# Second layer: the next heads' keys and values prepared in the middle of a unit instead of at its end, and half of the key copies moved to GpSimd

## The chip, the cores and the metric

The kernel runs on one core of one Trainium2 chip. The metric is the device time of one execution in microseconds, taken as the median of several runs. Beside these runs one execution was profiled; all rows below come from it.

## The reference

Two layers work on 1024 latent tokens and 256 context tokens of width 1024. The first (windowed attention and a gated MLP) is not touched here. The second is multi-head latent attention with 16 heads, and only the latent tokens go on from it:

```python
def mla_keys_values(kv_a, k_pe, kv_norm, w_kvb, row, col):
    kv = (rms_norm(kv_a, kv_norm) @ w_kvb).reshape(B_, L, C_HEADS, C_NOPE + C_V)
    k_nope, v = kv[..., :C_NOPE], kv[..., C_NOPE:]
    ...
    k = jnp.concatenate([k_nope, jnp.broadcast_to(k_pe, ...)], axis=-1)

def block_attention(q, k, v):          # 1024 queries, 1280 keys, 16 heads
    s = jnp.einsum('bqhd,bkhd->bhqk', qblk, k).astype(jnp.float32) * scale
    p = jax.nn.softmax(s, axis=-1)
    return jnp.einsum('bhqk,bkhd->bqhd', p, v)
```

Each head has 64 key columns of its own and 32 rotary ones that all heads share, and 64 value columns. All numbers are float32; a product is made of a high part and a rest (hi and lo) of each factor.

## The kernel before

The attention of the second layer is a loop over 64 **units** (plus three turns that finish late parts). A unit is one head and 256 queries: 8 head pairs, 4 query groups, 2 heads, so units 2m and 2m+1 share the queries of a group. Each turn of the loop walks through `ORDER1`, a list of short names, and each name puts its instructions at the end of each engine's queue. The order within TensorE, VectorE, ScalarE and GpSimd is this written order; the DMA queue of SyncE is ordered by the scheduler. The names, for unit n:

- S0 to S3: scores against the 1024 latent keys, into two PSUM tiles `s0` and `s1` of 1024 columns (one for each 128 queries, one buffer each). S4: scores against the context keys, into `sx`. K: the rotary part, added to `s0` and `s1`; it ends them.
- X0, X1, X2, P0, P1: VectorE takes the maxima of `s0`, `s1` and `sx` and makes the exponent's bias.
- E0 to E3: ScalarE's exponentials, from PSUM to `prob`. E0 reads `s0` and E1 reads `s1`, which frees them for the next unit.
- T0 to T4: TensorE transposes `prob` of the unit before, 512 columns at a time, into a PSUM bank called `tm`; a copy takes each to SBUF (`pt`). By `TURNS` T0 and T4 are copied by VectorE, the rest by ScalarE.
- A0, I, U, C: the products with the values and the normalisation, for earlier units.
- B and R (even units): queries of the next group, projected into a `tm` bank (B), then ScalarE makes `qa` from it and VectorE its rest (R).
- **D and L**: the preparation of later heads. `prep_pair` prepares the keys of the next head pair in four turns out of eight: the first splits the weights, the next three project 512, 512 and 256 columns (D) and evacuate them (L). `prep_v` prepares values for four heads in six turns out of sixteen: one splits weights, five project into a bank (D) and copy it out (L).

The tag `tm` has two banks. Transposes, B and D take them in turn, and whoever takes one waits for the readers of what lay there two allocations ago.

The keys of a head lie twice in `kh` (in partitions 0 to 63 and 64 to 127), and their rest once in `kl`, in a ring of two head pairs. In the evacuation of a key projection ScalarE copies the bank to both halves of `kh` for both heads, four copies, and VectorE subtracts `kh` from the bank to give `kl`, two operations.

Of the kernel before, what the change touches and what calls it, by code (L numbers as in the profile page):

```python
# [7 lines left out]
F32 = mybir.dt.float32  # L8
# [9 lines left out]
D = 1024  # L18
# [21 lines left out]

PAIR, VALUES = (2, 3, 4, 5, 8, 9, 11, 13), (1, 6, 7, 10, 12, 14)
WQ = 'VGG'
ORDER1 = 'S0 S1 T0 T1 I C S2 S3 K X0 T2 S4 T3 X2 P0 E0 B X1 P1 E2 R A0 E1 T4 D E3 U L'.split()
AVS = ((0, 5),), ((5, 10),)
TURNS = 'VAAAV'
KPE = {3: [0], 5: [1]}
# [6 lines left out]
class Kernel:  # L53
# [1083 lines left out]
    def prep_pair(self, hp):  # L1137

        nc, i, c1 = self.nc, self.i, self.c1
        raws = (self.raw(i["wkv_k"][:, hp * P:(hp + 1) * P].unsqueeze(1), [P, 1, P]), self.raw(i["wq_n"][hp], [P, 2, P]))  # L1140
        yield
        w = self.wsplit(c1, raws[0], 1, ("V", WQ[0]))
        self.wq[hp] = self.wsplit(c1, raws[1], 2, ("V", WQ[1]))
        yield
        ring = self.kring[hp % 2]
        kvh, kvl = self.kvh.unsqueeze(1), self.kvl.unsqueeze(1)
        for g0, gn in GROUPS:
            ps = self.project(w, self.split(kvh, kvl), g0, gn)
            yield
            c = slice(g0, g0 + gn)  # L1150
            src = [ps[64 * e:64 * e + 64] for e in range(2)]
            for e in range(2):
                for r in (0, 64):
                    nc.scalar.copy(ring[e][0][r:r + 64, c], src[e])  # L1154
            for e in range(2):
                nc.vector.tensor_tensor(ring[e][1][0:64, c], src[e], ring[e][0][0:64, c].bitcast(F32), op=ALU.subtract)  # L1156
            yield

    def prep_q(self, hp, qg):
# [25 lines left out]
    def layer1_attention(self):  # L1185
# [159 lines left out]
        with self.tc.manual_schedule(engines={E.PE, E.Activation, E.DVE, E.Pool}):  # L1345
            for n in range(N + 3):
                odd = n % 2
                for op in ORDER1:
                    o, a = op[0], int(op[1:] or 0)
# [255 lines left out]
```

## Time and profile before

| what | value |
|---|---|
| runs | 1546.64 to 1549.77 us, median of three 1547.48 us |
| the profiled execution | 1542.2 us, of which the span of the profile is 1540.3 us |
| TensorE matmul, busy share of the span | 1428.8 us, 93% |
| VectorE, ScalarE, GpSimd | 890.1 us (58%), 748.5 us (49%), 454.2 us (29%) |
| the 64 units of the second layer | K of the first at 810.8 us, K of the last at 1428.4 us |

The profile lists busy time for each engine, and for each group of instructions the idle time of its engine just before it with the instruction whose end released it. TensorE is the busiest by far, so its idle times in the loop, and the times at which its granted clock is below full speed, are what to look at first.

### The profile page before, as it was taken

To read this page: it belongs to the slowest core of one execution; us is meant where nothing else is said; L and a number is where in the kernel's file an instruction comes from. 1 tells how busy PE (TensorE), PEld (TensorE's weight loads), DVE (VectorE), ACT (ScalarE), POOL (GpSimd) and SP (SyncE) were. 2 spreads that over 40 slices of the span, in tenths; PEclk is the share of its full clock that TensorE was granted. 3 is DMA by queue.
4 is the path that set the end of the run, shared out by engine and by line. 5 is a ranking of instruction groups with operands and counts; after the bars stand their busy time and mean duration, and the time that the engine had idled before them with its cause. 6 is when DMAs were issued, how large, how long until landed. Compare 5 with 4: busy or idle time off the path is not lost.

```text
span 1540.3 us, 23388 instructions
## 1 busy us (share of the span) xinstructions
PE 1428.8 (93%) x8849; PEld 1103.3 (72%) x8849; DVE 890.1 (58%) x1692; ACT 748.5 (49%) x1580; POOL 454.2 (29%) x447
## 2 busy tenths in 40 slices
PE   6999999999998899999988898989898989899997
PEld 3767899777665577889866666766676667676776
DVE  5581134366667876534736665656666656577354
ACT  4422310256567544443336665756666666667321
POOL 4343133215557432331642121212121211224100
PEclk9999999999999999999999999999999999999999
DMA  8566311221214656140221010101011101212151
GB/s 338 228 229 255 106 34 30 89 96 57 79 56 151 185 148 197 55 128 30 94 93 47 25 34 24 44 21 33 29 33 32 34 22 35 70 41 91 59 186 69
DMA packets 91466, 138.96 MB, mean 90 GB/s; under 512 B 9089, under 2 KB 67657, under 8 KB 88281
## 3 DMA queue, kind: packets, MB, share of 16 engines
q1 hardware_dynamic: 91208, 137.21, 26.7%
q8 instruction: 69, 1.13, 0.3%
q14 instruction: 45, 0.36, 0.1%
q10 hardware_dynamic: 144, 0.26, 0.0%
HBM read 105.88 MB, written 31.56 MB: 89 GB/s over the span
## 4 chain that ended last, share of the span: by engine, by line
PE 41%; ACT 11%; DVE 4%; issue 4%; DMA 2%; POOL 1%; SPq 0%; DVEq 0%; POOLq 0%; ACTq 0%
PE tm L1275 9%; ACT prob L1265 5%; PE acc L1293 4%; PE s L99 3%; PE s L100 3%; PE s L101 3%; PE s L1227 3%; PE s L1228 3%; ACT kh L1154 3%; PE s L1239 2%; ACT pt L1282 1%; PE b L99 1%; PE b L101 1%; PE b L100 1%; DVE kl L1156 1%
## 5 line engine op out<-in xcount | busy, mean ns | idle before, releaser
L1275 PE MATMUL tm<-ident,prob 128*128 128x128 f32 x1280 | 197.2, 283 | 46.6 <-DVE kl L1156 44.9
L1275 PEld LDWEIGHTS tm<-ident,prob 128*128 128x128 f32 x1280 | 145.6, 142 | 102.0 <-issue 75.0
L1282 ACT COPY pt<-tm 128x512 f32<-128x512 f32 x192 | 112.9, 588 | 213.4 <-PE tm L1275 213.2
L1250 DVE TENSOR_REDUCE peak<-s 128x1 f32<-128x1024 f32 x128 | 156.1, 1219 | 50.3 <-PE s L1239 50.3
L1293 PE MATMUL acc<-pt,v 128*64 128x256 f32 x1280 | 152.9, 384 | 0.1
L1265 ACT ACTIVATE prob<-s,peak 128x1024 f32<-128x1024 f32 x128 | 142.7, 1114 | 12.6 <-DVE peak L1254 10.4
L1284 DVE COPY pt<-tm 128x512 f32<-128x512 f32 x128 | 88.4, 691 | 78.9 <-PE tm L1275 77.2
L1293 PEld LDWEIGHTS acc<-pt,v 128*64 128x64 f32 x1280 | 86.3, 136 | 47.3 <-issue 6.1
L1227 PE MATMUL s<-kh,qa 128*128 128x512 f32 x256 | 114.3, 447 | 5.9 <-ACT prob L1265 4.5
L91 POOL CAST qb<-qa 64x512 fp32r<-64x512 f32 x32 | 19.5, 608 | 319.7 <-ACT qa L1175 319.7
L95 POOL TENSOR_TENSOR w_lo<-raw,w_hi 128x512 fp32r<-128x512 f32 (+1 forms) x60 | 74.2, 1249 | 120.4 <-ACT w_hi L87 85.1
L1228 PE MATMUL s<-kl,qb 128*128 128x512 f32 x256 | 104.4, 408 | 0.0
L99 PE MATMUL b<-h,yh 128*128 128x512 f32 x160 | 64.0, 400 | 3.5 <-ACT yh L87 2.9
L99 PE MATMUL s<-h,w_hi 128*128 128x512 f32 x160 | 63.8, 412 | 2.2 <-ACT qk L379 2.2
L100 PE MATMUL s<-h,w_hi 128*128 128x512 f32 x160 | 63.7, 398 | 0.3 <-DVE h L95 0.3
L100 PE MATMUL b<-h,yh 128*128 128x512 f32 x160 | 63.3, 396 | 0.0
L101 PE MATMUL s<-h,w_lo 128*128 128x512 f32 x160 | 63.0, 395 | 0.0
L101 PE MATMUL b<-h,yl 128*128 128x512 f32 x160 | 62.4, 391 | 0.0
L1265 ACT ACTIVATE prob<-sx,peak 128x256 f32<-128x256 f32 x128 | 60.0, 469 | 0.0
L1227 PEld LDWEIGHTS s<-kh,qa 128*128 128x128 f32 x256 | 50.0, 195 | 13.6 <-ACT prob L1265 5.4
L1228 PEld LDWEIGHTS s<-kl,qb 128*128 128x128 f32 x256 | 50.4, 197 | 6.4
L745 DVE TENSOR_TENSOR pt<-pt,tm 128x512 f32<-128x512 f32 x68 | 42.4, 682 | 21.8 <-ACT mb L736 18.9
(473 smaller groups left out, 3750.4 us busy)
## 6 DMA issues: line engine op xcount, KB each, us to landing
wa<-in_w_ada_dram SPq DMA_DIRECT2D x16, 1024.0 KB, 8.1
x<-in_xs_dram SPq DMA_DIRECT2D x20, 512.0 KB, 6.1
raw<-in_w_dram SPq DMA_DIRECT2D x17, 512.0 KB, 4.0
wa<-in_w_adag_dram SPq DMA_DIRECT2D x8, 1024.0 KB, 6.5
pe<-pe_d SPq DMA_DIRECT2D x128, 64.0 KB, 2.0
raw<-in_w_out_dram SPq DMA_DIRECT2D x10, 512.0 KB, 3.8
yf<-y_d SPq DMA_DIRECT2D x10, 512.0 KB, 6.1
x_d<-x SPq DMA_DIRECT2D x8, 512.0 KB, 4.5
```

The lines of the kernel that those rows point to most:

```text
L95: e.tensor_tensor(lo, src, hi.bitcast(F32), op=ALU.subtract)
L99: mm(out, lhsT=ah, rhs=bh, start=start, stop=False)
L100: mm(out, lhsT=ah, rhs=bl, start=False, stop=False)
L101: mm(out, lhsT=al, rhs=bh, start=False, stop=stop)
L1227: mm(o, lhsT=qa[:, q], rhs=ka[:, k0:k1], start=True, stop=False)
L1228: mm(o, lhsT=qb[:, q], rhs=kb[:, k0:k1], start=False, stop=False)
L1250: nc.vector.reduce_max(m[:, 0, a:a + 1], banks[n, a], axis=AX.X)
L1265: nc.scalar.activation(probs[n][j][:, TL:T] if c else probs[n][j][:, 0:TL], src, AF.Exp, bias=peaks[n][:, 2, j:j + 1], scale=scale, accum_ ...
L1275: nc.tensor.transpose(tp[:, o * P:(o + 1) * P], probs[n][j][:, k * P:(k + 1) * P], self.ident)
L1282: nc.scalar.copy(dst, src)
L1284: nc.vector.tensor_copy(dst, src)
L1293: mm(accs[m][64 * e:64 * e + 64, 0:QG], lhsT=self.v4[hp // 2][:, kt, vc:vc + 64], rhs=pts[2 * m + e][:, kt], start=kt == 0, stop=kt == NT - 1)
```

## The change

In `ORDER1` D moves from behind T4 to between S2 and S3, and L moves from the end of the turn to behind K, ahead of the maxima. In the evacuation of a key projection ScalarE keeps the copies to the lower half of `kh`, one for each head; GpSimd copies the lower half to the upper half, from SBUF to SBUF, behind VectorE's two subtractions in the written order.

```diff
-ORDER1 = 'S0 S1 T0 T1 I C S2 S3 K X0 T2 S4 T3 X2 P0 E0 B X1 P1 E2 R A0 E1 T4 D E3 U L'.split()
+ORDER1 = 'S0 S1 T0 T1 I C S2 D S3 K L X0 T2 S4 T3 X2 P0 E0 B X1 P1 E2 R A0 E1 T4 E3 U'.split()
...
             for e in range(2):
-                for r in (0, 64):
-                    nc.scalar.copy(ring[e][0][r:r + 64, c], src[e])
+                nc.scalar.copy(ring[e][0][0:64, c], src[e])
             for e in range(2):
                 nc.vector.tensor_tensor(ring[e][1][0:64, c], src[e], ring[e][0][0:64, c].bitcast(F32), op=ALU.subtract)
+            for e in range(2):
+                self.hi("G", ring[e][0][64:128, c], ring[e][0][0:64, c].bitcast(F32))
             yield
```

TensorE's queue before, at the end of unit 3 (a unit with a key projection) and the start of unit 4: the last two of T4's four transposes, D into bank `tm_7698`, U, S0, and the transposes T0 and T1.

```order
L1275 MATMUL tm_7692<-ident,prob_7560 128x128
L1275 MATMUL tm_7692<-ident,prob_7561 128x128
L99 MATMUL tm_7698<-kvh,w_hi_7613 128x512
L100 MATMUL tm_7698<-kvl,w_hi_7613 128x512
L101 MATMUL tm_7698<-kvh,w_lo_7614 128x512
L1308 MATMUL acc_7590<-ident,spread_7640 128x128 x2
L1227 MATMUL s_1256_7712<-kh_7091,qa_7579 128x512
L1228 MATMUL s_1256_7712<-kl_7092,qb_7580 128x512
...
L1275 MATMUL tm_7718<-ident,prob_7675 128x128 x4
L1275 MATMUL tm_7724<-ident,prob_7675 128x128 x4
```

T1 of unit 4 (`tm_7724`) takes the bank that D (`tm_7698`) filled. The same projection in the changed kernel stands in the middle of unit 3, behind its T0, T1 and the first half of the scores for `s1`:

```order
L1276 MATMUL tm_7627<-ident,prob_7572 128x128 x4
L1276 MATMUL tm_7633<-ident,prob_7572 128x128 x4
L1228 MATMUL s_1247_7643<-kh_7093,qa_7427 128x512
L1229 MATMUL s_1247_7643<-kl_7094,qb_7428 128x512
L99 MATMUL tm_7646<-kvh,w_hi_7541 128x512
L100 MATMUL tm_7646<-kvl,w_hi_7541 128x512
L101 MATMUL tm_7646<-kvh,w_lo_7542 128x512
...
L1240 MATMUL s_1242_7621<-kc,qc_7429 128x512 x2
L1240 MATMUL s_1247_7643<-kc,qc_7429 128x512 x2
L1276 MATMUL tm_7664<-ident,prob_7573 128x128 x4
L1276 MATMUL tm_7677<-ident,prob_7573 128x128 x4
```

D (`tm_7646`) now takes the bank of T0 (`tm_7627`), T2 (`tm_7664`) that of T1, and T3 (`tm_7677`) takes the one that D filled.

VectorE's queue before, from the second projection of the same pair (unit 4): R's two operations, T4's copy, the two subtractions, T0's copy and the inverses of unit 5, then its maxima.

```order
L1177 TENSOR_TENSOR qa_7786<-tm_7776,qa_7786 64x256 x2
L1284 COPY pt_7717<-tm_7809 128x512
L1156 TENSOR_TENSOR kl_7365<-tm_7815,kh_7364 64x512
L1156 TENSOR_TENSOR kl_7367<-tm_7815,kh_7366 64x512
L1284 COPY pt_7831<-tm_7832 128x4x128
L1299 TENSOR_TENSOR total_7562<-total_7562 128x4
L1301 RECIPROCAL total_7562<-total_7562 128x4
L1250 TENSOR_REDUCE peak_7857<-s_1277_7826 128x1
```

And in the changed kernel, for the third projection (256 columns, unit 5): T0's copy, the inverses, the two subtractions, and the maxima behind them.

```order
L1285 COPY pt_7831<-tm_7832 128x4x128
L1300 TENSOR_TENSOR total_7574<-total_7574 128x4
L1302 RECIPROCAL total_7574<-total_7574 128x4
L1155 TENSOR_TENSOR kl_7365<-tm_7851,kh_7364 64x256
L1155 TENSOR_TENSOR kl_7367<-tm_7851,kh_7366 64x256
L1251 TENSOR_REDUCE peak_7867<-s_1277_7826 128x1
L1249 TENSOR_REDUCE peak_7867<-sx_7875 128x2
```

The subtractions stood behind the last copy of a unit; they now stand between its first copy and its first maximum.

## Rows read from the trace of the kernel before

**Rows 1.** Waits in 800 to 1430 us: engine line, releaser; us total, times, longest.

```profile
PE tm L1275 <- DVE kl L1156: 44.9, 21, 2.6
...
PE tm L99 <- DVE qa L1177: 7.1, 16, 0.5
```

**Rows 2.** Timeline of TensorE around one such wait: start us, us, instruction, [idle, releaser].

```profile
998.17 0.48 PE L99 MATMUL tm<-kvh,w_hi 128*128 128x512 f32 x1
...
1000.10 0.60 PE L1275 MATMUL tm<-ident,prob 128*128 128x128 f32 x4
1003.17 0.83 PE L1275 MATMUL tm<-ident,prob 128*128 128x128 f32 x4 [2.47 <-DVE kl L1156]
...
1004.22 0.63 PE L1228 MATMUL s<-kl,qb 128*128 128x512 f32 x1
```

**Rows 3.** Timeline of ScalarE there.

```profile
999.25 2.35 ACT L1154 CAST kh<-tm 64x512 fp32r<-64x512 f32 x4
```

**Rows 4.** Timeline of VectorE there.

```profile
1001.63 1.39 DVE L1156 TENSOR_TENSOR kl<-tm,kh 64x512 fp32r<-64x512 f32 x2 [2.49 <-ACT kh L1154]
```

**Rows 5.** K by its line: count, duration in ns (least/median/most), first and last start.

```profile
L1239 PE MATMUL s<-kc,qc x256: 489/497/792, 810.8 to 1428.4; 32*128 32x512 f32 x128
```

**Rows 6.** TensorE in units 15 to 17, which prepare no keys or values.

```profile
960.13 0.51 PE L1239 MATMUL s<-kc,qc 32*128 32x512 f32 x4
...
965.25 0.48 PE L1227 MATMUL s<-kh,qa 128*128 128x512 f32 x1
...
966.26 1.03 PE L1275 MATMUL tm<-ident,prob 128*128 128x128 f32 x8
...
967.60 0.39 PE L1227 MATMUL s<-kh,qa 128*128 128x512 f32 x1
...
968.15 0.51 PE L1239 MATMUL s<-kc,qc 32*128 32x512 f32 x4
...
969.80 0.60 PE L1275 MATMUL tm<-ident,prob 128*128 128x128 f32 x4
...
973.75 0.49 PE L1227 MATMUL s<-kh,qa 128*128 128x512 f32 x1
...
976.68 0.50 PE L1239 MATMUL s<-kc,qc 32*128 32x512 f32 x4
```

**Rows 7.** VectorE in unit 16.

```profile
966.90 0.69 DVE L1284 COPY pt<-tm 128x512 f32<-128x512 f32 x1 [0.89 <-PE tm L1275]
...
968.76 1.23 DVE L1250 TENSOR_REDUCE peak<-s 128x1 f32<-128x1024 f32 x1 [0.38 <-PE s L1239]
...
970.73 0.21 DVE L1254 TENSOR_SCALAR peak<-peak 128x1 f32<-128x1 f32 x1
...
973.44 0.86 DVE L1177 TENSOR_TENSOR qa<-tm,qa 64x256 fp32r<-64x256 f32 x2 [1.12 <-ACT qa L1175]
974.33 0.69 DVE L1284 COPY pt<-tm 128x512 f32<-128x512 f32 x1
```

**Rows 8.** ScalarE in unit 16.

```profile
971.06 1.12 ACT L1265 ACTIVATE prob<-s,peak 128x1024 f32<-128x1024 f32 x1
```

**Rows 9.** GpSimd in unit 16.

```profile
973.41 0.61 POOL L91 CAST qb<-qa 64x512 fp32r<-64x512 f32 x1 [8.78 <-ACT qa L1175]
```

**Rows 10.** VectorE and ScalarE around a 256-wide key slot (unit 21) and a value slot (22).

```profile
1027.77 0.86 DVE L1156 TENSOR_TENSOR kl<-tm,kh 64x256 fp32r<-64x256 f32 x2 [1.64 <-ACT kh L1154]
...
1026.23 1.50 ACT L1154 CAST kh<-tm 64x256 fp32r<-64x256 f32 x4
...
1037.54 0.59 ACT L1134 COPY v<-tm 128x512 f32<-128x512 f32 x1 [0.38 <-PE tm L101]
```

**Rows 11.** TensorE's projection of values in unit 22.

```profile
1036.56 0.35 PE L99 MATMUL tm<-wvh,kvh 128*128 128x256 f32 x1 [0.44 <-DVE qa L1177]
```

**Rows 12.** Stretches: length, busy us and count by engine, granted clock, DMA.

```profile
950.00:1050.00 100.00, 92.19 (x659) 68.66 (x658) 63.19 (x112) 61.23 (x137) 18.17 (x26) 0.97 0.10 31
...
1350.00:1400.00 50.00, 50.00 (x377) 37.73 (x375) 36.36 (x61) 36.05 (x81) 16.02 (x19) 1.00 0.20 59
```

## The prediction

> **What bounds the kernel now.** I read the page's shares first: TensorE is busy for nine tenths of the span, so the question is what it waits for in the second layer's loop. The list of waits for that stretch names two things that belong to the preparation of later heads [rows 1]: T1 waits for the subtractions `kl`, 44.9 us in 21 waits, and D itself waits for R's `qa`, 7.1 us in 16. The 21 are the key projections (7 head pairs, three each). The timeline of one of them shows why: TensorE has done T0 and stands 2.47 us before T1 [rows 2], because T1's bank is the one that D filled, and that bank is read last by `kl`, which starts only behind all four `kh` copies [rows 3, 4], which stand behind the four exponentials. The reader should see that `kl` starts 0.03 us after the last copy, not after the first one that it needs.
>
> How much the preparation costs in all comes from the starts of K. The first lies at 810.8 us, the last at 1428.4 [rows 5]: 617.6 us for 63 intervals. A unit that prepares nothing takes 8.02 us when odd and 8.53 when even [rows 6], together 32 x 8.53 + 31 x 8.02 = 521.6. A 512-wide key projection is three matmuls of 512 columns; four scores of that size take 1.01 us from S0 to T0 [rows 6], so three take 0.70 to 0.75, and I take 0.70. A value step streams as many columns; a 256-wide key projection half of them, 0.36: 14 x 0.70 + 15 x 0.70 + 7 x 0.36 = 22.8. That leaves 73 us; about 2 of it I put down to the loop's first and last units, which differ. So **71 us are lost around the preparation**: 52.0 listed waits; 37 x 0.2 = 7.4, since a wait costs more than is listed (T0 to T1 took 3.07 us [rows 2]; eight transposes and two scores take 1.34 and two scores 0.55 [rows 6], so four transposes need 0.40, and 2.67 was lost where 2.47 is listed); and 11.6 that remain. The remainder is TensorE's clock: behind the wait a score matmul takes 0.63 us where it takes 0.39 elsewhere [rows 2, 6], and the mean granted clock over 100 us of such units is 0.97, so between its two levels (1.2 and 2.4 GHz), against 1.00, the upper level throughout, where no keys are prepared [rows 12].
>
> **The change, part by part.** I replay a unit with times from S0's start, from unit 16 (S0 at 965.25): T0's copy ends at 2.34, the second half of the scores for `s1` starts at 2.35, K at 2.90, the first maximum 0.61 behind K, T3 at 4.55, the next S0 at 8.50 [rows 6, 7] (8.02 for an odd unit).
>
> *D between S2 and S3.* It takes T0's bank, so it waits for T0's copy. From the end of the last `kl` to T1 the trace has 0.15 us [rows 2, 4]; so D starts at 2.49, not 2.35: 0.14 lost in each of 36 slots with a projection. This is the least certain small term; from zero to 0.3.
>
> *512-wide keys (14 slots).* D takes 0.70, so K, T2, S4 and T3 come 0.84 later, T3 at 5.39. T3 now takes D's bank. From D's start to a reader on ScalarE is 0.98 us (1036.56 to 1037.54, same columns [rows 10, 11]): `kh` starts at 3.47, two copies at 0.59 end at 4.65 [rows 3], `kl` runs from 4.68 to 6.07 [rows 4], T3 starts at 6.22: **a wait of 0.83** in place of the old 2.5 to 2.6. The maxima are queued behind `kl`: X0 starts at 6.10, where 4.35 was possible. Its bias is ready 2.18 later (8.28) and E0, which in the trace starts about 0.1 behind the bias [rows 7, 8], has read `s0` at 8.38 + 1.12 = 9.5. The next S0 comes at 8.02 + 0.84 + 0.83 = 9.69 in an odd unit: the later maxima just fit. This is the cover, and it has under 0.1 us to spare when 0.15 is needed for the signal; each 0.1 more on the chain costs 1 us over ten odd units.
>
> *Four of the 14 are even*, with R. Its subtraction starts 2.38 behind E0 [rows 7, 8], at 10.76, ends at 11.62 and frees B's bank for the next T0 at 11.77; that T0 is due at 8.50 + 1.67 + 1.01 = 11.18, so 0.59 late, and T1 waits for T4's copy, which stands behind R's subtraction (0.69 and the signal: 12.49 against 12.17), 0.32 more. Such a unit loses 0.97 + 0.9.
>
> *256-wide keys (7 slots, all odd).* Two copies of 0.375 and two subtractions of 0.43 [rows 10]: T3's bank is free at 4.92, T3 is due at 5.05. Only D's 0.14 is lost. *Values (15 steps):* one copy, long before T3; 0.14 each. In even units the wait for `qa` goes, since D no longer takes B's bank.
>
> *GpSimd's copies* (48, two for each key projection) are read by the next head pair's first scores, two units or more later, and cost nothing on the path; ScalarE loses 48. GpSimd is idle 8.78 us in one stretch of a unit [rows 9], and a 64x512 copy takes 0.61 [rows 9]. R's work there now queues behind them; its results are due a unit later. Without that cover two copies would be 1.2 us. Two small things of about a microsecond and of opposite sign are left out: the seven weight splits that now stand ahead of the maxima, and the fewer copies for the first pair ahead of the loop. The weight loads are issued by SyncE well ahead in both programs.
>
> Sum of what is lost then: ten odd units 10 x 0.97 = 9.7, four even 4 x 1.9 = 7.5, the rest 22 x 0.14 = 3.1: 20.3 us. With waits of 0.8 I take the clock as full, since most of its loss follows the 2.5 us ones; at the other bound all 11.6 stay. **Gain 71 - 20 = 51 us**, 40 at that bound. The profiled execution took 1542.2 us, 5.3 under the median of the runs (1547.5); 51 off the first is 1491, and off the second 1497, which I give, since runs will be compared with runs.
>
> **The rivals.** *GpSimd and VectorE hold each other up.* The GpSimd copies start as `kl` does, with the same `kh` as input. If one excluded the other, `kl` and all behind it would come up to 2 x 0.61 = 1.2 us later in 14 slots, and about 0.5 in the seven narrow ones (two copies of half the length, less the 0.13 that T3 has there): 20 us, time 1517. Against it: R's subtraction, of the same form as `kl` (one input in PSUM, one in SBUF), takes 0.43 for 256 columns beside a GpSimd copy [rows 7, 9], and `kl` takes 0.43 for 256 columns with GpSimd idle [rows 10]. The Trainium skill speaks to this rival: by its page "SBUF — State Buffer" (section "Who interferes with whom") the port pair that VectorE shares with GpSimd is an exclusive lock, but a VectorE operation with at most one SBUF input, outside the two-port modes, doesn't take it. By the bare lock the time would be 1517, by the exemption 1497; the two rows agree with the exemption.
>
> *The waits keep the clock down.* Fourteen waits of 0.8 and four of 0.9, with part of the old loss left: 1497 + 6 to 12 = 1503 to 1509. For it: the clock's loss varies from slot to slot, so I can't read from where on it falls.
>
> *T3 hardly waits.* If `kl` starts behind its own head's copy, it ends 0.59 earlier, and T3 waits 0.24: 14 x 0.59 + 3 less, 1486. Against it is the start behind all copies [rows 3, 4].
>
> *Slower: the maxima come too late.* VectorE's queue is in order, so what holds `kl` holds X0, X1, E0 and E1, and the next S0 waits for `s0`. The place is the 21 key slots; the cover is used up in my replay, so from there each microsecond costs 21 us. It decides at 51/21 = 2.4 us beyond my X0: at 3 us the time is 1560. For it: 1.75 us of delay is certain. Against it: nothing in the queues ahead of `kl` waits for more than ScalarE's two copies.
>
> *The change does nothing measurable*: only by these cancelling.
>
> **How the numbers follow.** My sum 60 in 100 (its own range 1489 to 1504), the clock 14, GpSimd 9, T3 free 8, slower 5, cancelling 4. What a measurement of this kernel can tell from no change is about 0.2%, 3 us. So faster 0.92, same 0.03, slower 0.05. The range takes the first cases and the lower half of the GpSimd one: 1485 to 1516.
>
> **What would show it.** Right: the waits of T1 for `kl` gone, 14 waits of T3 for `kl` of about 0.6 listed; D's wait for `qa` gone, short waits of D for T0's copy; X0 starting right behind `kl`; S0 to S0 9.7 us in odd and 10.2 in even units with wide keys; granted clock at 0.99 or 1.00. Wrong: S0 waiting for E0 in these units, `kl` or GpSimd's copies longer than 0.70 and 0.61, or T2 waiting for ScalarE.

## The result and the profile after

The changed kernel takes 1487.16 us (median of four runs, 1485.86 to 1490.38), against 1547.06 us for the kernel before in the same comparison: a ratio of 0.961, with a 95% interval of 0.959 to 0.963. I had forecast 1497 with a range of 1485 to 1516. The direction, the waits removed and the clock were as forecast; one step, the wait that the change leaves behind, was not. The gain was 60 us where I gave 51.

The list of waits, TensorE alone, 800 to 1380 us, answers to [rows 1] (line numbers above 1157 are one higher than before; the kernel has one line more):

```profile
PE s L1228 <- ACT prob L1266: 6.1, 14, 1.9
PE tm L1276 <- DVE qa L1178: 3.4, 5, 0.8
PE tm L1276 <- ACT pt L1283: 1.6, 3, 0.8
...
PE tm L99 <- DVE kl L1155: 0.2, 1, 0.2
```

Both waits of [rows 1] are gone: T1 no longer waits for `kl`, nor D for `qa`. What is new is small: S0 waits for E0 (ten of these 14 follow odd units with wide keys, about 0.16 each; the other four, 4.5 us, lie at the loop's two ends, and the kernel before has them too), T0 for `qa` behind the four even ones. The waits of T3 for `kl` that I forecast are not in the list at all.

K by its line answers to [rows 5], and a stretch of units with key projections to [rows 12]:

```profile
L1240 PE MATMUL s<-kc,qc x256: 488/496/502, 809.7 to 1372.1; 32*128 32x512 f32 x128
```

```profile
840.00:940.00 100.00, 98.77 (x716) 72.75 (x716) 68.38 (x122) 68.13 (x147) 25.75 (x39) 1.00 0.12 35
```

The loop, from the first K to the last, takes 562.4 us where it took 617.6. Its bare work was 521.6 + 22.8 = 544.4 by the prediction's sum, so the loss around the preparation, with the loop's ends, fell from 73 to 18 us. The granted clock is 1.00 throughout such a stretch, the upper level. From the last K to the end of the span it is 112 us in both.

Unit 4, an even one with wide keys, shows the new order. TensorE (of unit 4 S0, S2, D, S3, T3 and B, then S0 and T0 of unit 5):

```profile
839.38 0.50 PE L1228 MATMUL s<-kh,qa 128*128 128x512 f32 x1 [0.16 <-ACT prob L1266]
...
841.20 0.48 PE L1228 MATMUL s<-kh,qa 128*128 128x512 f32 x1
...
841.79 0.50 PE L99 MATMUL tm<-kvh,w_hi 128*128 128x512 f32 x1
...
842.59 0.40 PE L1228 MATMUL s<-kh,qa 128*128 128x512 f32 x1
...
844.99 0.66 PE L1276 MATMUL tm<-ident,prob 128*128 128x128 f32 x4
845.79 0.39 PE L99 MATMUL tm<-qnh,w_hi 128*128 128x256 f32 x1 [0.15 <-DVE kl L1155]
...
849.42 0.48 PE L1228 MATMUL s<-kh,qa 128*128 128x512 f32 x1
...
851.32 1.29 PE L1276 MATMUL tm<-ident,prob 128*128 128x128 f32 x8 [0.73 <-DVE qa L1178]
```

ScalarE (the copies `kh`, T2's copy, E0):

```profile
843.13 1.19 ACT L1153 CAST kh<-tm 64x512 fp32r<-64x512 f32 x2
844.34 0.59 ACT L1283 COPY pt<-tm 128x512 f32<-128x512 f32 x1
...
847.94 1.11 ACT L1266 ACTIVATE prob<-s,peak 128x1024 f32<-128x1024 f32 x1 [1.67 <-DVE peak L1255]
```

VectorE (T0's copy, the subtractions, the first maximum):

```profile
841.05 0.69 DVE L1285 COPY pt<-tm 128x512 f32<-128x512 f32 x1 [1.04 <-PE tm L1276]
...
844.35 1.39 DVE L1155 TENSOR_TENSOR kl<-tm,kh 64x512 fp32r<-64x512 f32 x2 [1.82 <-ACT kh L1153]
845.77 1.23 DVE L1251 TENSOR_REDUCE peak<-s 128x1 f32<-128x1024 f32 x1
```

The chain is the forecast one: `kl` starts 0.03 us behind the second copy, the first maximum 0.03 behind `kl`, and E0 waits 1.67 us for its bias. But T3 starts at 844.99 while `kl` runs until 845.74. It follows T2's copy, which ends at 844.93. The one that waits for `kl` is B, at 845.79. So in this unit T3 is not given D's bank but T2's, and B gets D's. In all 14 units with wide keys T3 starts 0.47 us or more before `kl` ends; the strict turn of two banks that I described ahead of the prediction doesn't hold there.

### The profile page after: what moved, and what is told of

Read it like the earlier page. It is cut to its first block, busy times and chain, and to the rows that moved or that the text cites. A ratio compares the mean times of both kernels' runs of the same rounds, so it can differ in the third digit from the quotient of the medians.

```text
span 1484.1 us, 23403 instructions
## 1 busy us (share of the span) xinstructions
PE 1419.7 (96%) x8849; PEld 1092.8 (74%) x8849; DVE 884.6 (60%) x1692; ACT 726.6 (49%) x1532; POOL 479.2 (32%) x495
## 4 chain that ended last, share of the span: by engine, by line
PE 74%; DVE 8%; ACT 6%; issue 5%; DMA 4%; POOL 2%; SPq 0%; POOLq 0%; DVEq 0%; ACTq 0%
PE tm L1276 9%; PE acc L1294 7%; PE s L99 7%; PE s L100 7%; PE s L101 7%; PE b L99 5%; PE b L100 4%; PE b L101 4%; PE s L1228 4%; PE s L1229 3%; PE acc L773 2%; PE tm L99 2%; ACT prob L1266 1%; PE s L1240 1%; DVE kl L1155 1%
## 5 line engine op out<-in xcount | busy, mean ns | idle before, releaser
L1276 PE MATMUL tm<-ident,prob 128*128 128x128 f32 x1280 | 190.6, 279 | 5.1 <-DVE qa L1178 3.4
L1276 PEld LDWEIGHTS tm<-ident,prob 128*128 128x128 f32 x1280 | 141.9, 140 | 59.3 <-issue 22.8
L1229 PE MATMUL s<-kl,qb 128*128 128x512 f32 x256 | 101.1, 395 | 0.0
L751 ACT ACTIVATE pt<-pt 128x512 f32<-128x512 f32 x84 | 47.7, 625 | 13.3 <-DVE pt L745 13.3
```

The costliest lines, as they stand in the source:

```text
L1229: mm(o, lhsT=qb[:, q], rhs=kb[:, k0:k1], start=False, stop=False)
L1276: nc.tensor.transpose(tp[:, o * P:(o + 1) * P], probs[n][j][:, k * P:(k + 1) * P], self.ident)
```

## The experiments

**Only the order.** D and L move, ScalarE still makes four copies (the edit is shown against the changed kernel).

```diff
-                nc.scalar.copy(ring[e][0][0:64, c], src[e])
+                for r in (0, 64):
+                    nc.scalar.copy(ring[e][0][r:r + 64, c], src[e])
...
-            for e in range(2):
-                self.hi("G", ring[e][0][64:128, c], ring[e][0][0:64, c].bitcast(F32))
```

> Only the order is changed: D and L stand where the change puts them, but ScalarE still makes all four key copies. My theory (the gain is T1's wait for D's bank, given back in small by the chain bank, copies, subtractions, maxima, exponential) expects the chain to be 1.18 us longer in the 14 wide key slots and about 0.4 in the 7 narrow ones, so 19 us more than the changed kernel: 1506 us, S0 waiting for E0 by about 1.3 us in the odd wide slots. The rival (the place is everything, whoever copies) expects the changed kernel's 1487. The rival (GpSimd's copies are the gain) expects no less than 1535.

Measured: 1509.71 us, ratio 0.977 (0.975 to 0.978). TensorE's waits and ScalarE in unit 4:

```profile
PE tm L1275 <- ACT pt L1282: 13.8, 17, 1.2
PE s L1227 <- ACT prob L1265: 8.8, 14, 1.9
...
PE tm L1275 <- DVE kl L1156: 2.6, 7, 0.4
```

```profile
847.44 2.35 ACT L1154 CAST kh<-tm 64x512 fp32r<-64x512 f32 x4
849.82 0.58 ACT L1282 COPY pt<-tm 128x512 f32<-128x512 f32 x1
```

The size is the expected one (22 us over the changed kernel, 19 forecast), the place is not. T2's copy stands behind the four copies in ScalarE's queue, and T3, which needs T2's bank, waits for it: 13.8 us in 17 waits, of which three with 1.6 us lie at the loop's end and stand in the changed kernel too. S0's waits for E0 grow by 2.7 us. The seven waits for `kl` are T3's in the narrow slots (256-wide keys): there T3 does lie in D's bank.

**Only GpSimd.** The changed evacuation in the old order.

```diff
-ORDER1 = 'S0 S1 T0 T1 I C S2 D S3 K L X0 T2 S4 T3 X2 P0 E0 B X1 P1 E2 R A0 E1 T4 E3 U'.split()
+ORDER1 = 'S0 S1 T0 T1 I C S2 S3 K X0 T2 S4 T3 X2 P0 E0 B X1 P1 E2 R A0 E1 T4 D E3 U L'.split()
```

> Only the copies are changed: the old order, ScalarE two copies and GpSimd two. My theory expects T1's waits for the subtractions to fall by 1.18 us in 14 slots and 0.75 in 7, 22 us in all, and half or more of the clock's loss to go with them: 1515 to 1525 us, T1's waits 21 still there with 1.3 us each. The rival (the place is everything) expects 1547 or a few us less.

Measured: 1509.08 us, ratio 0.977 (0.975 to 0.978), so more than I expected. Its waits and its clock:

```profile
PE tm L1276 <- DVE kl L1155: 23.4, 21, 1.4
```

```profile
950.00:1050.00 100.00, 95.28 (x704) 71.35 (x702) 68.97 (x124) 62.72 (x141) 22.71 (x35) 1.00 0.11 33
```

T1's waits are all still there, but 23.4 us instead of 44.9: 21.5 less, where I expected 22. The rest is the clock: the same stretch of the kernel before had 0.97 [rows 12], this one 1.00, and its loop (813.7 to 1397.0) is 34.3 us shorter, 12.8 more than the waits. About 1 us of that stands in the loop's first unit, which has no keys to prepare (8.60 us from K to K before, 7.59 here, but 8.57 in a second run of the changed kernel). So 14 waits of 1.3 to 1.4 us and 7 of 0.7 leave the clock at its upper level over the whole loop, and the 11.6 us that the prediction put down to the clock come back with shorter waits.

In the kernel before, not every long wait lowered the clock. These are two stretches of it, each around the end of a wait of 2.45 us for `kl` (at 906.13 and 927.40), a part of the second, and then the loop with only GpSimd:

```profile
905.00:915.00 10.00, 8.43 (x64) 6.41 (x65) 7.43 (x13) 5.84 (x14) 0.61 (x1) 1.00 0.09 28
926.00:936.00 10.00, 8.60 (x56) 6.33 (x56) 6.50 (x11) 4.45 (x10) 0.37 (x1) 0.83 0.10 29
929.00:931.00 2.00, 2.00 (x10) 1.29 (x10) 0.89 (x1) 0.00 (x0) 0.00 (x0) 0.50 0.20 66
```

```profile
813.70:1397.00 583.30, 546.78 (x4002) 409.17 (x4001) 396.43 (x689) 373.37 (x831) 148.28 (x213) 1.00 0.13 41
```

In the loop of the kernel before the clock falls to the lower level (0.50) nine times: once in the first unit, and eight times at or within 1 us behind one of the 14 waits of wide slots (2.45 to 2.60 us), never at the seven of narrow slots (1.4). Each part of the change alone gives some 34 us in the loop, both give 55: the clock's part is to be had only once.

**L behind the first maximum.**

```diff
-... S3 K L X0 T2 ...
+... S3 K X0 L T2 ...
```

> The changed kernel with L behind X0 instead of ahead of it, so VectorE takes the first maximum before the subtractions. If D's bank goes to B or T4, as the trace of the changed kernel suggests, and what is left is lost because E0 comes late, this gives E0 0.6 us earlier in 14 slots: S0's waits for E0 vanish (4 us), the late T0 behind even wide slots shrinks (2 us), B waits 0.6 us longer in four slots (2 us): about 1483 us. If T3 were held by D's bank, as my prediction had it, T3 would wait for subtractions that end 0.6 us later: 1495 us or more.

Measured: 1488.02 us, ratio 0.963 (0.961 to 0.964), no gain. TensorE and VectorE in unit 4:

```profile
847.51 0.66 PE L1276 MATMUL tm<-ident,prob 128*128 128x128 f32 x4
848.81 0.39 PE L99 MATMUL tm<-qnh,w_hi 128*128 128x256 f32 x1 [0.65 <-DVE kl L1155]
```

```profile
846.24 1.23 DVE L1251 TENSOR_REDUCE peak<-s 128x1 f32<-128x1024 f32 x1 [1.18 <-PE s L1240]
847.38 1.38 DVE L1155 TENSOR_TENSOR kl<-tm,kh 64x512 fp32r<-64x512 f32 x2
```

T3 starts 1.2 us before `kl` ends, and B waits for it: in the wide slots of even units the bank is settled. The effect on the wide slots was as expected: from K to K an odd one takes 9.17 us instead of 9.48 (10 of them), an even one 10.16 instead of 10.44 (4). But units with the weight split got 0.28 longer (7) and narrow ones 0.18 (7); together 0.8 us less, not the 4 I gave it. The step that I missed is that L is not only the wide evacuation.

**Copy and subtraction in turn.**

```diff
             for e in range(2):
                 nc.scalar.copy(ring[e][0][0:64, c], src[e])
-            for e in range(2):
                 nc.vector.tensor_tensor(...)
```

> The changed kernel with copy and subtraction written in turn for the two heads: copy, subtraction, copy, subtraction. If a subtraction only has to wait for the end of a run of copies, the first starts 0.59 us earlier and the chain ends 0.59 us earlier: about 1482 us. If ScalarE and VectorE take turns at a PSUM bank (the second copy then stands behind the first subtraction), the chain is as long as before or 0.1 us longer: 1487 to 1490 us, and the second copy is seen to start behind the first subtraction.

Measured: 1488.55 us, ratio 0.963 (0.962 to 0.965). ScalarE, then VectorE, in unit 4:

```profile
846.22 0.58 ACT L1153 CAST kh<-tm 64x512 fp32r<-64x512 f32 x1
847.54 0.58 ACT L1153 CAST kh<-tm 64x512 fp32r<-64x512 f32 x1 [0.75 <-DVE kl L1154]
```

```profile
846.83 0.68 DVE L1154 TENSOR_TENSOR kl<-tm,kh 64x512 fp32r<-64x512 f32 x1 [1.21 <-ACT kh L1153]
848.16 0.69 DVE L1154 TENSOR_TENSOR kl<-tm,kh 64x512 fp32r<-64x512 f32 x1 [0.65 <-ACT kh L1153]
```

The second copy of ScalarE, which needs nothing from VectorE, waits for the first subtraction. The two engines take turns at the bank, so the chain is as long as in the changed kernel (2.63 us from the first copy to the last subtraction, there 2.61). It also fits that `kl` stood behind all four copies [rows 3, 4].

The Trainium skill ("PSUM — Partial Sum Buffer", section "PSUM bank collisions raise a hardware error") says that the compiler's scheduler lets no two engines touch one bank and quadrant of 32 partitions together, reads included, while different quadrants may be accessed at once. By that rule the second copy, which reads partitions 64 to 127, would not have to wait for the first subtraction, which reads 0 to 63. Here it does (0.75 us of idling): in this kernel the turn covers the whole bank.

**The changed kernel again, and GpSimd's copies made twice.** A control for the runs that follow, and the price of GpSimd's load.

> The changed kernel again, beside the other kernels of this call: 1487 us, within 2 us.

> The changed kernel with GpSimd's copies made twice, 96 instead of 48, 26 us more of its work in the loop. My theory (its copies lie beside other work and neither hold VectorE nor are waited for) expects the changed kernel's time, within 2 us. The rival that GpSimd and VectorE hold each other up expects the subtractions or the maxima behind them to come up to 1.2 us later in the wide slots: 10 to 20 us more.

```diff
+            for e in range(2):
+                self.hi("G", ring[e][0][64:128, c], ring[e][0][0:64, c].bitcast(F32))
```

Measured: 1488.73 us (ratio 0.963, 0.961 to 0.965) for the control, 1488.0 us (0.962, 0.961 to 0.964) with twice the copies. GpSimd and VectorE of the latter in unit 4:

```profile
847.49 2.33 POOL L91 CAST kh<-kh 64x512 fp32r<-64x512 f32 x4 [7.45 <-ACT kh L1153]
```

```profile
848.06 1.39 DVE L1155 TENSOR_TENSOR kl<-tm,kh 64x512 fp32r<-64x512 f32 x2 [1.81 <-ACT kh L1153]
849.48 1.23 DVE L1253 TENSOR_REDUCE peak<-s 128x1 f32<-128x1024 f32 x1
```

The subtractions lie wholly beside GpSimd's four copies and take 1.39 us, as they did with GpSimd idle [rows 4]. The rival falls.

**L by slot, and then wide keys in odd units alone.** The first takes L behind X0 in wide slots only:

```diff
-ORDER1 = '... S3 K L X0 T2 ...'
+ORDER1 = '... S3 K L X0 M T2 ...'
...
+                    elif o in "LM":
+                        wide = n % 16 in PAIR and n // 8 < 7 and PAIR.index(n % 16) % 4 in (1, 2)
+                        if (o == "M") == wide:
+                            for p in preps:
+                                next(p, None)
```

> The changed kernel with L behind X0 in the 14 slots with wide keys alone, and ahead of X0 in the others. The run with L behind X0 everywhere showed wide slots 0.31 us (odd) and 0.28 us (even) shorter, and weight-split and narrow slots 0.28 and 0.17 us longer. If these are separate, this keeps the first and drops the second: 4 us under the changed kernel, 1483 us. If the chain of one slot carries into the next, no gain: 1487.

The second also changes the turns:

```diff
-PAIR, VALUES = (2, 3, 4, 5, 8, 9, 11, 13), (1, 6, 7, 10, 12, 14)
+PAIR, VALUES = (2, 3, 5, 7, 8, 9, 11, 13), (1, 4, 6, 10, 12, 14)
```

> As the kernel with L placed by slot, and the second and third key projections of the first four-head half moved from units 4 and 5 to units 5 and 7, a value step from 6 to 4 and one from 7 to 6, so that no wide key projection lies in an even unit, where R's query work stands behind the maxima. An even wide slot lost 1.3 us there beyond its matmuls and an odd one 0.44: 4 x 0.8 = 3 us less, 1480 us. If the loss of the even slots comes from B's bank and is carried on by the value step that now stands there, nothing is gained: 1483.

Measured: 1484.47 us (ratio 0.9605, 0.9588 to 0.9622) and 1480.78 us (0.958, 0.9565 to 0.9595), against 1488.73 (0.9629, 0.9613 to 0.9646) for the changed kernel beside them. K by its line, in the control, with L by slot, and with wide keys in odd units:

```profile
L1240 PE MATMUL s<-kc,qc x256: 488/497/502, 811.9 to 1375.3; 32*128 32x512 f32 x128
```

```profile
L1240 PE MATMUL s<-kc,qc x256: 488/497/502, 814.3 to 1373.5; 32*128 32x512 f32 x128
```

```profile
L1240 PE MATMUL s<-kc,qc x256: 488/496/502, 812.6 to 1368.3; 32*128 32x512 f32 x128
```

The loops are 563.4, 559.2 and 555.7 us: 4.2 less for the first step (4 expected), 3.5 less for the second (3 expected). The last is faster than the kernel before and than the changed one, with an interval that does not touch the control's; between the first step and the control the intervals overlap, and the loop's length carries the claim: from K to K the ten odd wide slots take 9.18 us in it and 9.50 in the control, the four even ones 10.16 and 10.43.

## Why the prediction was right, and where it was off

*The wait to be removed.* Right in place and size: 44.9 and 7.1 us of listed waits are gone, and the loop lost 73 us before and 18 after. The gain in the loop is 55 us where I gave 51.

*The clock.* Right, and shown by GpSimd's part alone: the clock came back in full though 21 waits remained, 14 of them of over a microsecond. My other bound, that all 11.6 us stay, and the rival that short waits keep the clock down fall.

*The step that failed* is "T3 now takes D's bank". It holds in the seven narrow slots and not in the 14 wide ones. In a narrow one (unit 13: `kl`, T2's copy, T3) T3 starts while T2's copy still reads its bank, so it lies in the other, which `kl` has left:

```profile
927.34 0.86 DVE L1155 TENSOR_TENSOR kl<-tm,kh 64x256 fp32r<-64x256 f32 x2 [1.23 <-ACT kh L1153]
...
928.04 0.59 ACT L1283 COPY pt<-tm 128x512 f32<-128x512 f32 x1 [0.73 <-PE tm L1276]
...
928.56 0.60 PE L1276 MATMUL tm<-ident,prob 128*128 128x128 f32 x4
```

In the wide slots T3 takes T2's bank, and in even units B takes the one that D filled (odd units have no B, and who takes it there is not shown). So the wait of 0.83 us for `kl` does not exist. With D's own delay it made 0.97 us per odd wide slot; measured from K to K such a slot loses 0.75 (9.48 - 8.03 - 0.70): 0.15 at D, about 0.2 at T3, which starts some 0.06 us behind the end of T2's copy, and the rest at S0. The next S0 starts 0.54 us behind the start of U in unit 9, a wide slot, and 0.13 behind it in unit 15, which prepares nothing (U and S0 of each):

```profile
894.69 0.38 PE L1309 MATMUL acc<-ident,spread 128*128 128x128 f32 x2
895.23 0.50 PE L1228 MATMUL s<-kh,qa 128*128 128x512 f32 x1 [0.16 <-ACT prob L1266]
...
949.28 0.38 PE L1309 MATMUL acc<-ident,spread 128*128 128x128 f32 x2
949.41 0.48 PE L1228 MATMUL s<-kh,qa 128*128 128x512 f32 x1
```

With T3 nearly on time S0 is due earlier, and E0, late by the chain as forecast, is what it waits for: the cover of "under 0.1 us" needed the wait that isn't there. S0 waiting for E0 is one of the signs of being wrong that I named. The chain was sized rightly, and the place of its wait was wrong. That my loss per slot came near the measured one is in part luck, since one loss stands in for another.

*The rival "T3 hardly waits"* gave 1486, nearer to the result than my 1497, but not by its own mechanism: `kl` does start behind both copies (844.35, 0.03 us behind the second), and T3 is free because it lies in another bank.

*Even wide slots:* right in kind. T0 waits 0.73 us for `qa`; a slot loses some 1.5 us beyond its matmuls (10.37 - 8.53 - 0.36 in three of the four), where I gave 1.9.

*D's wait for T0's copy* costs about 0.04 us, not 0.14 (without D the second half of the scores follows at 0.55 us behind S2's first matmul, D comes at 0.59). But a wide D takes 0.80 us (841.79 to 842.59), not the 0.70 that I took. The two errors cancel, and value and narrow slots lose 0.14 to 0.16 from K to K, so my sum for them held. With 0.75 and 1.5 in place of 0.97 and 1.9 the sum of what is lost is about 17 us instead of 20.

*GpSimd* costs nothing, twice its copies neither. *Slower:* this rival's mechanism, S0 held by E0, is there, but in small: the maxima are late by as much as I worked out, and the price was about 0.4 us per odd wide slot; it needed maxima 2.4 us later than mine to undo the gain.

*The rest of the gap.* Between the two profiled executions the gain is 1542.2 - 1485.9 = 56.3 us: 55.2 in the loop, 1.1 ahead of it. That last bit is not the change's for certain, as the first K lies between 809.7 and 814.3 us in the runs here. Nor is 1 us of the loop's first unit: the control's loop is 54.2 us shorter than that of before. Between the medians the gain is 59.9, and 56.7 between the control and the kernel before beside it. I had carried the difference of 5.3 us between the profiled execution of before and its median over to the changed kernel, whose runs lie within 1.3 us of its profiled one at the median. Why the runs of the kernel before lie higher above its profiled one stays open. The clock may be a part of it: beside the later experiments the kernel before took from 1542.30 to 1548.65 us, the first with a mean granted clock of 0.984, as in the profiled execution, and all above 1546 with 0.979 to 0.982. But one of 1543.70 has 0.982 too.

## What to carry to other kernels

When an engine waits for a buffer, look for what stands ahead of the buffer's last reader on that reader's queue: here each of two remedies, reading earlier in the order and fewer operations ahead, brought 34 us of the 55. Waits that also lower TensorE's clock are worth more than their listed time, and whichever remedy comes first collects that. An evacuation moved ahead of other work gives its delay to that work, so look where that has slack, slot by slot: the same move was worth 0.3 us in one kind of unit and cost 0.28 in another.

## What was not expected of the hardware

Between the transposes T0 and T1, waits of TensorE of up to 1.4 us left the granted clock at 1.00. Of the 14 of 2.45 to 2.60 us in the kernel before, eight brought it to the lower level and six did not, which gave 0.95 to 0.98 over stretches of 100 us. What tells the eight from the six stays open. A GpSimd copy of 64x512 float32 from SBUF to SBUF took 0.58 to 0.61 us, as long as ScalarE's copy of that size out of PSUM (0.59).
